# Attention in written order beside the product pairs: shared inner keys, narrower scores, raw zs

## The chip, the cores and the metric

The kernel runs on one core of one Trainium2 chip. What counts is the device time of one execution in microseconds (us), the median of the runs. TensorE is called PE (its weight loads PEld), VectorE DVE, ScalarE ACT, GpSimd POOL and SyncE SP, as the profile does. SBUF is the memory on the chip that all engines use; PSUM is the small memory of 8 banks into which PE writes; DRAM is outside.

## The reference, cut to what matters

One layer on 1024 tokens of width 1024, in float32. `h` is the normalised input; one projection gives queries `q` (16 heads of 64), keys `k` and values `v` (2 groups), and the gate inputs `za`, `u`, `vs`, `zs`, `gm`.

```python
a = window_sink_attention(q, k, v, att_sinks[l])
a = (a * jax.nn.silu(za)) @ w_att_out[l]
sgo = chunked_spatial_gating(gelu(u), gelu(vs), ...)
sgo = (sgo * jax.nn.silu(zs)) @ w_sg_out[l]
ga, gs = jnp.split(jax.nn.sigmoid(gm + b_merge[l]), N_BRANCHES, axis=-1)
x = x + (ga * a + gs * sgo) @ w_o[l]
```

In the attention each chunk of 64 queries sees its own 64 keys and the 128 before them, 192 in all; a learned sink per head joins the maximum and the denominator. A tile of 128 tokens holds two chunks: keys 0 to 191 of its window of 256 belong to the first, 64 to 255 to the second. So the 128 keys in the middle are seen by both, and the outer 64 on each side by one. In the first tile (t = 0) there is nothing before, and the chunks see 64 and 128 keys.

## The kernel before, in words

Everything is held transposed, features by tokens. Each product in float32 is made of three fp32r matmuls: an operand is split into a rounded part `hi` (a cast on ACT, L153) and a rest `lo` (a subtraction on DVE, L154), and `product` (L331) adds hi x hi, hi x lo and lo x hi over four blocks of 128: 12 matmuls of 512 columns.

Two blocks of 128 output features make a *pair* (`gemm_pair`, L348). A pair is a 2 x 2 block product with seven products instead of eight, named after their right-hand forms: `b11`, `t1`, `t2`, `b21`, `t3`, `b22`, `t4`. It needs seven left-hand blocks: the weights themselves (0, 1, 6) and four sums of them (2 to 5). Those sums are made on DVE (`sums`, L233) or, for some pairs, in DRAM by POOL's adding DMAs (`early_job`, L288). `split_next` (L206) splits the next unit of two blocks while the pair runs, four times a pair; a job's loads are issued by `begin_job` (L200). Results leave as four quarters, each through `finish`.

There are 33 pairs in this order: u (4), k and v (1), q (4), zs (4), the gates gs (4) and ga (4), za (4), the two output projections (8); then four pairs by tokens. The attention lies beside eleven of them: the last three of zs, and gs and ga. It has 32 steps, `steps` (L984): 2 key groups, 8 tiles, 2 parities of the heads, four heads each.

A step has three parts.

- `softmax_stage` (L1083): per chunk four score matmuls (two heads pairs, two parts of the split keys) over all 256 keys of the window into a bank `sc`; the minimum of the negated scores on DVE (L1106, L1107); four exponentials on ACT with their sums (L1109); the sink's; the reciprocal; and the scaling of the weights, half on DVE (L1128), half on ACT (L1130).
- `weight_stage` (L1133): per chunk and head pair one transpose of the first 128 keys (L1150) and one of the last 64 (L1161): 8 a step, 4 at t = 0; then splits of both banks `tp`.
- `value_stage` (L1166): per chunk two matmuls of 256 columns for the first 128 keys (hi and lo) and one for the last 64 (hi and lo stacked), L1183; the bank `o` is then put into `aT` by a copy on ACT (L1189) and an addition on DVE (L1190).

The order: `attention` (L1196) is a generator that yields after each part, and the pairs' hooks, seven a pair, call it by a credit (L1236). This only sets the order in which the program is traced; the framework's scheduler then orders the instructions of every engine itself, by that order as priority and by its own estimate of when each is ready, and gives out the buffers. Loads are issued on SP's queue, and stores too; POOL's queue carries `at_dr`, the adding DMAs (paced by L281 to follow an eviction) and some stores.

PSUM has two banks each of `mm`, `o`, `tp` and `sc`. In a pair `mm` holds the accumulator, `o` holds `t5` and `t2`, and the attention's values need `o` too.

zs: `zs_pair` (L1037) runs a pair, then applies Silu to its four quarters after the last exponentials traced so far (L1055 to L1060), loads the mixed rows `s1_dr`, multiplies on DVE (L1065) and stores `s_dr`, the input of the first output projection. Its forms are made on DVE and ACT (`forms_of`, L1306) at the end of za, whose pairs (L1336) apply Silu to their quarters, multiply by the attention `at_dr` and store `a_dr`.

## Time and profile before

| what | us |
|---|---|
| median of three runs (all: 937.09, 937.17, 937.66) | 937.17 |
| profiled execution, first to last instruction (span) | 935.4 |
| what a run has beside the span (937.17 - 935.4) | 1.8 |
| PE busy in it | 913.1 |
| DVE busy | 685.7 |
| ACT busy | 529.0 |
| first product of the eleven interleaved pairs to first of za | 320.4 to 618.7 |

The profile gives the span of the one execution that it took, not that execution's time as a run; the 1.8 us beside it are what the median has more. In a row of the timeline stand the start, the length, engine, line, operation, what is written and read, and how many were merged; in a row of a group the count, then busy us and the mean ns of one, then the engine's idle time before it and what ended it. A matmul's length contains its way through the array, so neighbours overlap, and the pace is read from starts.

### The profile page before, as it was taken

How to read it: one execution, taken by the hardware profiler on the slowest of the kernel's cores; microseconds unless marked ns; L12 is line 12 of the kernel's file. 1: busy time of each engine (PE TensorE's matmuls, PEld its weight loads, DVE VectorE, ACT ScalarE, POOL GpSimd, SP SyncE). 2: the span in 40 equal slices, each digit the busy share in tenths (PEclk: the TensorE clock that was granted, in tenths of full speed). 3: DMA queues.
4: the chain of work that ended last, by engine and by line, in shares of the span. 5: the costliest groups of instructions: out<-in, count | busy, mean ns of one | idle time of the engine just before them, and what ended most of it. 6: DMA issues, size and time to landing. Idle time of an engine off the chain costs nothing.

```text
span 935.4 us, 13276 instructions
## 1 busy us (share of the span) xinstructions
PE 913.1 (98%) x4393; PEld 758.6 (81%) x4393; DVE 685.7 (73%) x1214; ACT 529.0 (57%) x1031; POOL 128.2 (14%) x189
## 2 busy tenths in 40 slices
PE   7999999999999989999999999999999999999996
PEld 5788888888888778888888888888887887888885
DVE  5784776646678688787877877756598589679996
ACT  6873433334445468777757667744475475468443
POOL 1002222213011001111111111001110110210012
PEclk9999999999999999999999999999999999999998
DMA  6237679887788778897777778849668754998623
GB/s 251 99 113 212 215 183 190 163 156 220 240 282 265 222 231 220 186 229 195 207 217 240 242 176 231 235 162 371 234 207 313 268 202 155 293 307 289 204 101 124
DMA packets 129196, 202.24 MB, mean 216 GB/s; under 512 B 12680, under 2 KB 61064, under 8 KB 129128
## 3 DMA queue, kind: packets, MB, share of 16 engines
q1 hardware_dynamic: 109976, 148.69, 48.2%
q0 software_dynamic: 19008, 52.44, 23.7%
q8 instruction: 35, 0.57, 0.2%
q14 instruction: 33, 0.27, 0.1%
q10 hardware_dynamic: 144, 0.26, 0.1%
HBM read 144.59 MB, written 86.11 MB: 247 GB/s over the span
## 4 chain that ended last, share of the span: by engine, by line
PE 69%; DVE 15%; DMA 7%; issue 4%; ACT 3%; SPq 1%; POOL 0%; DVEq 0%; ACTq 0%
PE ps_mm L339 29%; PE ps_o L339 20%; PE ps_mm L564 5%; DVE wl L154 3%; PE ps_tp L339 2%; PE ps_sc L1098 2%; PE ps_o L1183 2%; DMA wr<-in_w_dram 2%; PE ps_tp L564 1%; PE ps_sc L564 1%; PE ps_o L564 1%; PE ps_tp L757 1%; DVE bq L183 1%; PE ps_tp L1150 1%; PE ps_tp L1161 1%
## 5 line engine op out<-in xcount | busy, mean ns | idle before, releaser
L153 ACT CAST wh<-s 128x1024 fp32r<-128x1024 f32 (+1 forms) x78 | 78.1, 1004 | 89.0 <-PE ps_mm L339 39.5
L153 ACT CAST wh<-wr 128x1024 fp32r<-128x1024 f32 (+1 forms) x80 | 66.3, 830 | 86.7 <-PE ps_mm L339 35.1
L154 DVE TENSOR_TENSOR wl<-wr,wh 128x1024 fp32r<-128x1024 f32 (+1 forms) x80 | 75.6, 947 | 51.4 <-ACT wh L153 51.0
L154 DVE TENSOR_TENSOR wl<-s,wh 128x1024 fp32r<-128x1024 f32 (+1 forms) x78 | 91.0, 1166 | 15.5 <-ACT wh L153 14.3
L1109 ACT ACTIVATE pr<-ps_sc,sm 128x192 f32<-128x192 f32 (+2 forms) x128 | 51.1, 411 | 33.8 <-DVE sm L1107 29.9
L339 PE MATMUL ps_o<-T_b22h,wh 128*128 128x512 f32 x148 | 59.0, 399 | 1.6 <-ACT x L361 1.6
L339 PE MATMUL ps_o<-T_t1h,wh 128*128 128x512 f32 x148 | 58.7, 396 | 0.3 <-ACT wh L153 0.2
L339 PE MATMUL ps_o<-T_b22l,wh 128*128 128x512 f32 x148 | 57.9, 391 | 0.0
L339 PE MATMUL ps_o<-T_b22h,wl 128*128 128x512 f32 x148 | 57.8, 390 | 0.0
L339 PE MATMUL ps_o<-T_t1h,wl 128*128 128x512 f32 x148 | 57.7, 390 | 0.0
L339 PE MATMUL ps_o<-T_t1l,wh 128*128 128x512 f32 x148 | 57.6, 390 | 0.0
L339 PE MATMUL ps_mm<-T_b11h,wl 128*128 128x512 f32 x140 | 54.8, 392 | 2.0 <-DVE wl L154 2.0
L339 PE MATMUL ps_mm<-T_t4h,wh 128*128 128x512 f32 x140 | 55.5, 397 | 0.7 <-DVE x L374 0.7
L339 PE MATMUL ps_mm<-T_t3h,wh 128*128 128x512 f32 x140 | 55.3, 395 | 0.0
L339 PE MATMUL ps_mm<-T_b11h,wh 128*128 128x512 f32 x140 | 55.1, 394 | 0.0
L339 PE MATMUL ps_mm<-T_t2h,wh 128*128 128x512 f32 x140 | 54.8, 392 | 0.0
L339 PE MATMUL ps_mm<-T_t4h,wl 128*128 128x512 f32 x140 | 54.7, 391 | 0.0
L339 PE MATMUL ps_mm<-T_t3h,wl 128*128 128x512 f32 x140 | 54.6, 390 | 0.0
L339 PE MATMUL ps_mm<-T_b11l,wh 128*128 128x512 f32 x140 | 54.6, 390 | 0.0
L339 PE MATMUL ps_mm<-T_t4l,wh 128*128 128x512 f32 x140 | 54.6, 390 | 0.0
L339 PE MATMUL ps_mm<-T_t2h,wl 128*128 128x512 f32 x140 | 54.6, 390 | 0.0
L339 PE MATMUL ps_mm<-T_t3l,wh 128*128 128x512 f32 x140 | 54.6, 390 | 0.0
(353 smaller groups left out, 2436.0 us busy)
## 6 DMA issues: line engine op xcount, KB each, us to landing
wr<-in_w_dram SPq DMA_DIRECT2D x86, 256.0 KB
sums<-in_w_dram POOLq DMA_DIRECT2D x20, 512.0 KB, 5.4
s<-sums SPq DMA_DIRECT2D x20, 512.0 KB
s_dr<-x SPq DMA_DIRECT2D x32, 256.0 KB
q_hl<-qhl SPq DMA_DIRECT2D x16, 512.0 KB
q<-q_hl SPq DMA_DIRECT2D x64, 128.0 KB
wr<-in_w_dram SPq DMA_DIRECT2D x14, 512.0 KB
y_dr<-x POOLq DMA_DIRECT2D x28, 256.0 KB, 6.3
```

Source lines behind the costliest of these rows:

```text
L153: nc.scalar.copy(hi, src)
L154: return nc.vector.tensor_sub(lo, src, hi.bitcast(F32))
L183: op(dst[:, i : i + 2, :], a[:, i : i + 2, :], c[:, i : i + 2, :])
L339: nc.tensor.matmul(acc, lt, rt, start=fresh and k == 0 and n == 0, stop=k == 3 and n == 2, skip_group_check=True,)
L564: mm = nc.tensor.matmul(acc, lt, rt, start=k == 0 and n == 0, stop=k == KC - 1 and n == 2)
L757: nc.tensor.matmul(pm[:, t * P : (t + 1) * P], xh[:, half * 4 + t, g * P : (g + 1) * P], bias[-1][1][:, g % 4, :], start=True, stop=True,)
L1098: nc.tensor.matmul(sc[:, i, k0:], q_of[:, c, i * P : (i + 1) * P], kt[:, f, k0:], start=f == 0, stop=f == 1,)
L1109: nc.scalar.activation(pr[:, c, i, 0 : hi - lo], sc[:, i, lo:hi], AF.Exp, bias=nmax[:, c, i : i + 1], scale=-1.0, accum_out=sums[:, c, i : ...
L1150: nc.tensor.transpose(pt[:, at : at + P], pr[:, c, i, 0:P], ident[:])
L1161: nc.tensor.transpose(pt[0:64, at : at + P], pr[:, c, i, first : first + 64], ident[:])
L1183: nc.tensor.matmul(po[:, cs], lt, rt, start=n == 0, stop=n == len(terms) - 1)
```

## The change

1. **Written order.** In the eleven pairs `locked_pair` replaces `gemm_pair` and the generator. Inside `tc.manual_schedule` PE, ACT and DVE run their instructions as written; SP and POOL are still scheduled. With a, b, c, d for four steps in a row (d is the next pair's a), PE's order in a pair is: values of the step before a, `b11`, transposes of a, scores of b, `t1`, values of a, `t2`, transposes of b, `b21`, scores of c, `t3`, values of b, `b22`, transposes of c, scores of d, `t4`.
2. **Shared inner keys.** The weights of both chunks lie in one tile of 384 columns per head pair. The 128 inner keys are transposed four times (two chunks, two head pairs) into one bank, and the outer keys of both chunks, side by side, twice into another. The values are two matmuls of 512 columns for the inner keys and one of 256 per chunk for the outer.
3. **192 keys of scores.** A score matmul covers only its chunk's 192 keys (64 and 128 at t = 0, as columns of the window).
4. **zs raw.** The three zs pairs store their quarters unchanged in `zr_dr`. In the first two za pairs `gate_raw` loads six rows of it with `s1_dr`, applies Silu on ACT, multiplies on POOL and stores `s_dr`; the s quarters are loaded from za's third pair on instead of the second, one each hook instead of every second. The first zs pair still multiplies on DVE, but applies Silu at once, quarter by quarter.
5. **Weight sums.** gs and ga (8 jobs) and the first two of each output projection get their sums from DRAM; za's and the third and fourth of the first projection's are now made on DVE. DVE's sums are made in two halves, at places of their own. Locked pairs split a pair's third unit inside that pair rather than ahead of it.
6. **Queues.** The `a_dr` stores of za's first two pairs go on SP's queue, not POOL's.

```diff
+        ends = mtile([P, 2, 3 * HD], F32R, "v", 2, aheads)
+        k = max(t - 1, 0) * P
+        both = rows[k : (t + 1) * P].rearrange("(c p) d -> p c d", p=64)
         for e in range(2):
-            nc.sync.dma_start(vb[e * 64 : (e + 1) * 64].bitcast(F32), own)
+            nc.sync.dma_start(ends[e * 64 : (e + 1) * 64].bitcast(F32), both[:, :: both.shape[1] - 1, :])
...
                     nc.tensor.matmul(
-                        sc[:, i, k0:],
+                        sc[:, i, lo:hi],
                         q_of[:, c, i * P : (i + 1) * P],
-                        kt[:, f, k0:],
+                        kt[:, f, lo:hi],
...
+    def turn(n):
+        st = held[n]
+        st.wide = wide = P if st.t else 64
+        st.inner = bank("tp")
         for c in range(2):
+            for i in range(2):
+                at = (2 * c + i) * P
+                nc.tensor.transpose(
+                    st.inner[0:wide, at : at + P], st.pr[:, i, place_of(c, 64 if st.t else P, 192)], ident[:]
+                )
+        st.ends = bank("tp")
+        for i in range(2):
+            nc.tensor.transpose(st.ends[0:wide, i * P : (i + 1) * P], st.pr[:, i, P : P + wide], ident[:])
...
+        if st.t:
+            terms = [(inner[:, vs], st.a[:, i, :], slice(0, HALF)) for i in range(2)]
+        else:
+            terms = [(ends[:, 0, vs], st.a[:], slice(0, HALF))]
+        for c in range(0 if st.t else 1, 2):
+            terms.append((ends[:, c, vs], st.b[:, cols(c)], cols(c)))
...
+        of(values, a - 1)
+        acc = bank("mm")[:]
+        mm(acc, 0, "b11", True)
+        of(weigh, a)
+        for tail in tails:
+            tail()
+        tails.clear()
+        of(outputs, a - 1)
+        if p:
+            make_sums(None, 1)
+        if by_dve and p:
+            begin_job()
+
+        of(turn, a)
+        of(scores, b)
+        t5 = bank("o")[:]
+        mm(t5, 2, "t1", True)
+        x11 = xtile()
+        pace[0] = nc.scalar.copy(x11[:], acc)
+        of(casts, a)
+        of(inner_rest, a)
+        of(maxima, b, 0)
+        of(ends_rest, a)
+        of(maxima, b, 1)
+        of(exponentials, b)
+
+        of(values, a)
+        mm(acc, 3, "t2", False)
+        of(weigh, b)
+        of(outputs, a)
+        x22 = xtile()
+        pace[0] = nc.scalar.mul(x22[:], t5, -1.0)
+        if p:
+            split_next()
+            if not by_dve:
+                begin_job()
+
+        of(turn, b)
+        t2 = bank("o")[:]
+        mm(t2, 1, "b21", True)
+        x12 = xtile()
+        pace[0] = nc.scalar.copy(x12[:], acc)
+        of(casts, b)
+        of(inner_rest, b)
+        of(ends_rest, b)
+        split_next()
+        make_sums(None, 1 if p else 2)
+
+        of(scores, c)
+        mm(acc, 4, "t3", False)
+        nc.vector.tensor_add(x11[:], x11[:], t2)
+        finish(0, 0, x11, x11[:], 1.0)
+        of(maxima, c, 0)
+        of(maxima, c, 1)
+        split_next()
+        of(exponentials, c)
+
+        of(values, b)
+        mm(t5, 5, "b22", False)
+        of(weigh, c)
+        nc.vector.tensor_sub(x22[:], x22[:], acc)
+        finish(1, 1, x22, x22[:], 1.0)
+        of(outputs, b)
+
+        of(turn, c)
+        of(scores, d)
+        mm(acc, 6, "t4", False)
+        nc.vector.tensor_add(x12[:], x12[:], t5)
+        finish(0, 1, x12, x12[:], 1.0)
+        hold = split_next(True)
+        of(casts, c)
+        of(inner_rest, c)
+        of(maxima, d, 0)
+        of(ends_rest, c)
+        of(maxima, d, 1)
+        hold()
+        of(exponentials, d)
+        tails.append(lambda: finish(1, 0, xtile(), acc, -1.0))
...
+    with tc.manual_schedule(engines={mybir.EngineType.PE, mybir.EngineType.Activation, mybir.EngineType.DVE}):
+        p = 0
+        for dst in (zr_dr, gs_dr, ga_dr):
+            for m in range(2 if dst is zr_dr else 0, KC, 2):
+                locked_pair(p, rest(dst, m))
+                p += 1
...
+        for j in range(2, KC):
+            yield
+            z = raws.pop(j)
+            nc.scalar.activation(z[:, 0:2, :], z[:, 0:2, :], AF.Silu)
+            if j + 3 < KC:
+                load_raw(j + 3)
+            yield
+            nc.gpsimd.tensor_tensor(z[:, 0:2, :], z[:, 0:2, :], z[:, 2:4, :], op=ALU.mult)
+            copy_to(s_dr[j * P : (j + 1) * P, :], z[:, 0:2, :].rearrange("p h n -> p (h n)"))
```

`weigh` is the scaling of the weights with what leads to it, `maxima` the minima on DVE, `exponentials` ACT's part; `casts` makes the hi parts of both transposed banks (one cast for the inner keys, one of 64 partitions for each chunk's outer ones), `inner_rest` and `ends_rest` the lo parts; `outputs` puts the values' bank into `aT`. `split_next(True)` makes only the cast and hands back the subtraction, to be placed later (`hold()`).

More of the change, by code (lines that the diff above doesn't have):

```diff
@@ L1166, in value_stage @@
[L1166 to L1188 removed]
+                    nc.scalar.mul(v, v, st.inv[:, c, i : i + 1])
@@ new lines, in ends_of, with casts @@
+    def ends_of(st):
+        return ((1, slice(0, 64), slice(64, P)), (0, slice(64, P), slice(0, 64)))[: 2 if st.t else 1]
+    def casts(n):
+        st = held[n]
+        if st.t:
+            st.a = atile([P, 2, HALF], F32R, "pT", 2)
+            nc.scalar.copy(st.a[:, 0, :], st.inner[:])
+        else:
+            st.a = atile([P, HALF], F32R, "pT", 2)
+            nc.scalar.copy(st.a[0:64, :], st.inner[0:64, :])
+        st.b = atile([P, HALF], F32R, "pTb", 2)
+        for c, hi, lo in ends_of(st):
+            nc.scalar.copy(st.b[hi, cols(c)], st.ends[hi, 0:256])
@@ new lines, in outputs, with locked_pair, of, mm @@
+                st.at[:],
+            )
+            if n + 3 < len(steps):
+                value_loads(*steps[n + 3][:2])
+        del held[n]
+    held = {}
+    tails = []
+    def locked_pair(p, finish):
+        a, b, c, d = range(3 * p - 1, 3 * p + 3)
+        def of(make, n, *rest):
+            if 0 <= n < len(steps):
+                make(n, *rest)
+        def mm(acc, at, form, fresh):
+            product(acc, ready[n, at], hb[form], fresh)
+            part_of_early(1 if p < 3 else 2)
+        n = done[0]
+        done[0] += 1
+        by_dve = n + 1 not in ahead_of
+        of(values, a - 1)
[70 more added lines that the diff above has]
+        tails.append(lambda: finish(1, 0, xtile(), acc, -1.0))
@@ L1251, in hybrid_tile @@
+    begin_job()
     assert not early
@@ L1338, in hybrid_tile @@
             want_gates(at_dr, m)
-        if m == 2:
+            next(gating)
+        if m == 4:
+            for _ in gating:
+                pass
             s_q = {}
```

357 lines of the change are left out of this document (168 added, 189 removed).

## The prediction

> **What bounds the kernel now.** The page first: which engine has no room, and at what clock.
>
> ```profile
> span 935.4 us, 13276 instructions
> ...
> PE 913.1 (98%) x4393; PEld 758.6 (81%) x4393; DVE 685.7 (73%) x1214; ACT 529.0 (57%) x1031; POOL 128.2 (14%) x189
> ...
> PEclk9999999999999999999999999999999999999998
> ```
>
> PE is busy 98% of the span at the full clock in every slice; DVE and ACT have about a quarter and two fifths to spare. A busy share may hide waiting, so next the busy time by stretch. The first row is the eleven interleaved pairs (the first `T_b11h` of the second zs pair to the first one of za), the next two are za's four pairs; the columns are length, busy us (and instructions) of PE, PEld, DVE, ACT and POOL, clock, DMA share, GB/s. The last row is the fullest DMA stretch I found.
>
> ```profile
> 320.40:618.70 298.30, 293.78 (x1599) 249.66 (x1598) 231.18 (x519) 209.67 (x557) 36.61 (x47) 1.00 0.77 214
> 618.70:656.80 38.10, 38.10 (x170) 31.55 (x169) 20.23 (x25) 16.39 (x24) 4.03 (x7) 1.00 0.86 310
> 656.80:694.90 38.10, 38.10 (x170) 31.53 (x169) 25.17 (x30) 23.45 (x31) 4.30 (x8) 1.00 0.60 205
> 640.00:645.00 5.00, 5.00 (x23) 4.13 (x23) 3.89 (x4) 1.19 (x2) 0.07 (x1) 1.00 1.04 407
> ```
>
> DVE works 231 and ACT 210 of 298.3 us in the eleven pairs, so there PE is the limit as long as the order of the work lets it run. What PE's time consists of is read from the chain of work that ended last and from PE's timeline, by distances between starts (a matmul's own duration overlaps the next one's).
>
> ```profile
> 112.22 2.72 PE ps_o L339 x12
> ```
>
> Twelve 512-wide matmuls, one product, take 2.72 us. Eleven pairs of seven products: 77 x 2.72 = 209.4 us. The attention's instructions, in the timeline of the step near 504 us:
>
> ```profile
> 504.40 0.60 PE L1150 MATMUL ps_tp<-ident,pr 128*128 128x128 f32 x4
> 504.84 0.60 PE L1161 MATMUL ps_tp<-ident,pr 128*64 128x128 f32 x4
> 505.19 1.21 PE L1098 MATMUL ps_sc<-k,q 128*128 128x256 f32 x8
> 506.24 0.40 PE L339 MATMUL ps_mm<-T_t4h,wh 128*128 128x512 f32 x1
> ```
>
> Four transposes take 504.84 - 504.40 = 0.44, so 0.109 each. From 504.40 to the next product's start at 506.24 is 1.84; without eight transposes (0.87) it leaves 0.97 for eight 256-wide score matmuls, 0.121 each. Value matmuls (256 wide), and score matmuls of a first tile (128 wide):
>
> ```profile
> 347.64 0.28 PE L1183 MATMUL ps_o<-pTb,v 128*128 128x256 f32 x1
> 347.76 0.40 PE L1183 MATMUL ps_o<-pT,v 128*128 128x256 f32 x2
> 348.00 0.39 PE L339 MATMUL ps_mm<-T_b11h,wh 128*128 128x512 f32 x1
> ```
>
> ```profile
> 322.66 1.05 PE L1098 MATMUL ps_sc<-k,q 128*128 128x128 f32 x8
> 323.55 0.45 PE L339 MATMUL ps_o<-T_t1h,wh 128*128 128x512 f32 x1
> ```
>
> The values: 0.36 for three, 0.120 each. The narrow scores: 0.89 for eight, 0.111 each: half the columns, almost the same time.
>
> There are 32 steps (2 key groups x 8 tiles x 2), 4 of them with t = 0. Now: scores 28 x 8 x 0.121 + 4 x 8 x 0.111 = 30.7; values (28 x 6 + 4 x 3) x 0.120 = 21.6; transposes (28 x 8 + 4 x 4) x 0.109 = 26.2; together 78.5. So 298.3 - 209.4 - 78.5 = **10.4 us are neither**: waiting and the change from one kind of matmul to another. The waits of PE's weight loads name most of it (us, times, longest):
>
> ```profile
> PEld ps_o L339 <- DVE aT L1190: 3.7, 6, 1.3
> PEld ps_o L339 <- ACT x L361: 2.0, 1, 2.0
> PEld ps_o L1183 <- DVE x L369: 1.9, 6, 0.5
> PEld ps_sc L1098 <- ACT pr L1109: 1.5, 4, 1.0
> ```
>
> These are banks held by `aT` and `x` evictions, and exponentials that come late.
>
> **The change, part by part.** *Less PE work.* The 128 keys that both chunks see are turned once for two 256-column blocks that lie side by side, and the two outer 64-key blocks share one transpose per head pair: 6 transposes a step instead of 8 (6 instead of 4 at t = 0), so 32 x 6 x 0.109 = 20.9, a gain of 5.3. The values become two 512-wide and two 256-wide matmuls a step (one and one at t = 0): a 512-wide one is 2.72 / 12 = 0.227, so 60 x 0.227 + 60 x 0.120 = 20.8, a gain of 0.8. The scores go from 256 to 192 columns. The trace has no 192; its bounds are the 256-wide row (0.121, no gain) and the 128-wide one (0.111, a gain of 224 x 0.010 = 2.2). I take 0.118, a gain of 0.7, since halving the columns gave so little. Sum: 78.5 - 6.8 = 71.7.
>
> The Trainium skill bears on this ("TensorE: Matmul & The Clock Gate", section "Back-to-back issue gap"): an isolated warm matmul needs N / 2.4 + 2.5 ns, thus 82.5 for 192 columns and 109 for 256, which would make the scores' gain 6.0 us by an estimate from that page. This case's trace disagrees, 111 ns where the formula gives 56 for 128 columns; the same page's section "LDWEIGHTS" (128 columns at 1.2 GHz, 107 ns) agrees with it.
>
> *The written order.* PE, ACT and DVE now run the eleven pairs in a fixed order, three steps a pair: a pair's PE work is 7 x 2.72 + 3 x 2.29 = 25.9. The question is what PE waits for. Between a step's scores S and its transposes T the order puts two products and one step's values (2 x 0.227 + 2 x 0.120 = 0.69): 6.13 us, for each of the three steps. In that time its softmax must pass DVE and ACT. One softmax now, DVE then ACT:
>
> ```profile
> 462.64 1.03 DVE L1106 TENSOR_REDUCE sm<-ps_sc 128x2 f32<-128x384 f32 x2 [0.18 <-PE ps_sc L1098]
> 465.69 0.16 DVE L1120 TENSOR_TENSOR sm<-sm,sm 128x4 f32<-128x4 f32 x1 [1.62 <-ACT sm L1119]
> 466.10 0.55 DVE L1128 TENSOR_SCALAR pr<-pr,sm 128x192 f32<-128x192 f32 x2
> ```
>
> ```profile
> 463.84 0.42 ACT L1109 ACTIVATE pr<-ps_sc,sm 128x192 f32<-128x192 f32 x1 [1.07 <-DVE sm L1107]
> ...
> 465.44 0.22 ACT L1119 ACTIVATE sm<-sm 128x4 f32<-128x4 f32 x1
> ...
> 466.16 0.80 ACT L1130 ACTIVATE pr<-pr,sm 128x192 f32<-128x192 f32 x2
> ```
>
> From 462.64 to 466.16 + 0.80 it takes 4.3. What else stands on these queues in the gap, with its price:
>
> ```profile
> L154 DVE TENSOR_TENSOR wl<-s,wh 128x1024 fp32r<-128x1024 f32 x24 | 29.3, 1222 | 7.1 <-ACT wh L153 5.9 <-PE ps_sc L1098 1.1
> L154 DVE TENSOR_TENSOR pT<-ps_tp,pT 128x512 fp32r<-128x512 f32 x28 | 19.2, 685 | 1.9 <-ACT pT L153 1.6
> L369 DVE TENSOR_TENSOR x<-x,ps_o 128x512 f32<-128x512 f32 x11 | 7.5, 685 | 1.6 <-PE ps_o L339 1.2
> L240 DVE TENSOR_TENSOR s<-wr 128x512 f32<-128x512 f32 x10 | 6.8, 682 | 0.0
> L154 DVE TENSOR_TENSOR pTb<-ps_tp,pTb 64x256 fp32r<-64x256 f32 x4 | 1.7, 418 | 0.1
> ```
>
> ```profile
> L153 ACT CAST wh<-s 128x1024 fp32r<-128x1024 f32 x24 | 25.1, 1045 | 15.2 <-PE ps_mm L339 8.2 <-PE ps_o L339 6.3 <-DVE s L241 0.6
> L153 ACT CAST pT<-ps_tp 128x512 fp32r<-128x512 f32 x28 | 16.4, 586 | 1.7 <-PE ps_tp L1150 1.4
> L1055 ACT ACT_TABLE_LOAD x4 | 5.1, 1283 | 0.1
> L1109 ACT ACT_TABLE_LOAD x4 | 5.1, 1283 | 0.9 <-DMA s_dr<-x 0.4 <-DVE sm L1107 0.4
> ```
>
> Step b: the previous step's inner rest (0.69) ahead and its two outer rests (2 x 0.42) between the two minima: 4.3 + 1.5 = 5.8 of 6.13. Step c: the term into `x11` (0.69) ahead: 5.0; ACT's split of 1.05 falls beside the minima. Step d: inner rest, outer rests, and on ACT the held split (1.05) and three casts (0.59 + 2 x 0.38), of which some precede S: 5.8 to 6.5. So the waits lie between 0 and 0.4 us a step. Whole queues fit: DVE about 20 of 25.9 a pair, ACT about 19.6. In the first two pairs and the last, DVE also makes weight sums (0.68 each, two to four a pair); in the other eight they now come from DRAM, made by POOL's adding DMAs, which takes 8 x 2.7 us off DVE and adds about 0.75 MB of loads a pair at a DMA share of 0.77. Eight ACT table loads (10.2 us of ACT, the two last rows) shrink to the one from Silu to Exp, since no Silu is left among the exponentials; the zs results go straight out and hold no `x` tile for a gate. PE did not wait for ACT's throughput, so I count this only as part of the waits. I take 0.2 us a step, 6.4 in all, between 0 and 0.8 (a step's chain that overruns its gap by 0.4 twice). **Stage: 209.4 + 71.7 + 6.4 = 287.5, a gain of 10.8.**
>
> *What is moved to za.* Six raw rows are loaded (1 MB each with `s1`), passed through Silu on ACT (1.05 each, ACT has 16.4 of 38.1 in use), multiplied on POOL and stored. POOL's price of such a multiply is not in the trace; the nearest row is a subtract of the same size:
>
> ```profile
> 8.98 2.37 POOL L580 TENSOR_TENSOR T_t1l<-T_t3h,T_t1h 128x1024 fp32r<-128x1024 f32 x1 [7.53 <-ACT T_t1h L579]
> ```
>
> 6 x 2.4 = 14.2 of 38.1 us: POOL has the room, and nobody waits for it but the s quarters, which load a pair later than now, all four in the first four hooks of za's third pair. DVE also makes za's sums, 2.7 a pair, beside 20.2 of 38.1. The stores of `a_dr` move from POOL's queue to SP's, where the raw loads, the gates and the next weights stand behind a store that waits for DVE; a late weight has a whole pair of cover (its split is needed 11 us into the pair, its product at 19). DMA in the first two za pairs: 6 MB raw, 3 stored, 2 gates, 2 of `a_dr`, 2 weights = 15 MB in 38.1 us = 394 GB/s, against 310 now and 407 in the fullest stretch. It just fits, so the price lies between 0 and, if the quarters come 5 us late and the s forms with them, 5. I take 1.0.
>
> Before the eleven pairs the sums are only split in two and the order of POOL's early DMAs changes; PE has no wait there to lose, and I count nothing (cover: the DVE's idle quarter; without it 0.7 a product).
>
> *Sum.* The profiled execution has a span of 935.4, and the median of the three runs, 937.17, lies 1.8 above it. -10.8 + 1.0 = -9.8: span 925.6, **927.4 us**.
>
> **The rivals.**
>
> *Clean order*: the gaps hold and PE changes over for nothing: remainder 0 to 2, stage about 282.5, gain 15.8: 922.4 with the 1.0 of za. For it: no chain above is longer than its gap by more than 0.4. Against it: S, T and V are many small groups, and today a remainder stays too where nothing is named.
>
> *Scores by their columns*: if only columns counted, 192 of them would take 192 / 512 x 0.227 = 0.085, a gain of 224 x 0.036 = 8.1 instead of 0.7: 920.0. Against it is the 128-wide row, 0.111 where columns alone would make it 0.057; nothing in the trace is for it. (This is what the issue-gap rule of the Trainium skill's page, named above, would do here.)
>
> *Late s forms*: za at its DMA limit costs the 5, so 931.4. For it: 394 of 407 GB/s. Against it: the quarters are first cast when za's last pair has freed its forms, a pair after their issue. The Trainium skill has a rule against POOL's multiply ("SBUF — State Buffer", section "Who interferes with whom"): a DVE instruction with two SBUF inputs and a GpSimd one that reads SBUF shut each other out for their whole length. No run here shows the pair. As a mechanism of this kernel it takes up to 14.2 us from DVE in those two pairs, 20.2 + 5.5 + 14.2 = 39.9 of 38.1: DVE becomes their limit by about 2 us, and the result is 929 to 930, within this rival.
>
> *The order is too tight* (slower): the chain S to T runs through some six hand-overs between DVE and ACT in fixed queues, and an instruction that comes late (a weight that has not landed ahead of the exponentials, a bank not free) delays every one behind it; the scheduled order of before could put other work there. Place: the gap from the fourth scores (before `t4`) to their transposes in the next pair. It decides where a step waits more than (298.3 - 1.0 - 281.1) / 32 = 0.51 us; at 0.7 the stage takes 303.5: 943.4.
>
> *Narrow scores are slow*: two passes per column below 256, so 192 columns at 2 x 192 / 512 x 0.227 = 0.170 instead of 0.121: +11.0 against no gain, +11.7 against my sum: 939.1. Against it the first narrow score of a tile, whose weights were already in:
>
> ```profile
> 322.66 0.22 PE L1098 MATMUL ps_sc<-k,q 128*128 128x128 f32 x1
> ```
>
> 0.22 against 0.28 for 256 and 0.39 for 512 columns: one rate for all widths, so the floor is the weight load, not the column.
>
> **Chances.** Forecast (924.5 to 930): 0.48. Late forms (930 to 935.3): 0.14. Clean order (below 924.5): 0.14. Scores by columns: 0.02. Too tight an order: 0.15, narrow scores: 0.03. Gains and losses that cancel: 0.04. A measurement of this kernel can tell 0.2% (1.9 us) from no change, so faster 0.78, same 0.04, slower 0.18. The range takes in the clean order down to 921 and reaches up to 940, past the break-even and the cheaper of the two slow cases, with about 0.09 left above and 0.09 below.
>
> **What would show it.** Right: transposes 192 at 0.109; 192-wide scores eight in 0.94; from the first product of the eleven pairs to the first of za 284 to 291 us; at most two or three table loads there. The order fails if PE's waits name `pr` (the scaled weights) or `aT` dozens of times, or a split ahead of the exponentials waits for a `wr` or `s` DMA. Za fails if PE's wait at the first sg pair (now 1.7 us at 712 to 715) grows, with the first cast of a form ended by a DMA. I am wrong altogether if the pair's length, 25.9 and some tenths, is not what the middle pairs show.

## The result: slower by 0.6%, and the profile after

| | before | after |
|---|---|---|
| median of four runs, us | 937.41 (937.09 to 938.25) | 942.44 (940.39 to 946.31) |
| span of the profiled execution, us | 935.4 | 938.4 |

The ratio is 1.0057, 95% interval 1.0034 to 1.0080: slower, outside the forecast's 924.5 to 930 and outside its range. A profile shows one execution, for the changed kernel the shortest of its four (940.39 us) and, among the experiments below, for the multiply on DVE, no late gating and no gating at all the longest, so a span or a wait of one trace need not be the median's: 3.0 us between the spans stand here for 5.0 between the medians. The page of the profile after, the rows that answer to those of before:

```profile
span 938.4 us, 13120 instructions
...
PE 909.4 (97%) x4285; PEld 751.4 (80%) x4285; DVE 691.8 (74%) x1222; ACT 529.7 (56%) x1050; POOL 150.3 (16%) x199
...
PEclk9999999999999999999999999999999999999998
```

PE is less busy by 3.7 us and the span is longer by 3.0: PE waits more, and part of the busy time is spent at a lower clock. Where, is seen in busy time by stretch. The eleven pairs begin in both traces with the first `b11` product at 316.1; the first row is theirs before, the second after (to za's first product), the next two are za's four pairs, the last two stretches of 5 us with a lowered clock.

```profile
316.10:618.70 302.60, 297.34 (x1613) 252.22 (x1613) 235.48 (x528) 211.40 (x559) 36.61 (x47) 1.00 0.76 213
```

```profile
316.10:612.60 296.50, 290.21 (x1505) 244.89 (x1504) 223.41 (x515) 204.91 (x570) 43.20 (x57) 0.99 0.87 236
612.60:657.60 45.00, 40.41 (x170) 32.04 (x168) 26.57 (x28) 21.51 (x29) 16.66 (x7) 0.96 0.92 340
657.60:697.70 40.10, 39.10 (x169) 31.42 (x170) 33.21 (x39) 23.46 (x31) 3.33 (x6) 1.00 0.84 300
320.00:325.00 5.00, 2.99 (x8) 2.30 (x9) 5.00 (x11) 2.04 (x4) 0.00 (x0) 0.75 0.57 182
635.00:640.00 5.00, 4.68 (x13) 3.28 (x14) 5.00 (x5) 1.43 (x2) 2.39 (x1) 0.66 0.99 342
```

The eleven pairs: 302.6 to 296.5, a gain of 6.1 where 10.8 was forecast (302.6 is more than the prediction's 298.3 because the stretch begins 4.3 us earlier: the last product of the first zs pair, `t4`, lies inside it in both traces). Za's four pairs: 76.2 (two rows of 38.1 before) to 85.1, a loss of 8.9 where 1.0 was forecast. -6.1 + 8.9 is +2.8, nearly the 3.0 of the spans.

*Inside the eleven pairs* the forecast pace is there. A step in PE's timeline, its six transposes, eight scores and the next product:

```profile
503.37 0.60 PE L1180 MATMUL ps_tp<-ident,pr 128*128 128x128 f32 x4
503.80 0.38 PE L1185 MATMUL ps_tp<-ident,pr 128*128 128x128 f32 x2
503.94 1.17 PE L1109 MATMUL ps_sc<-k,q 128*128 128x192 f32 x8
504.95 0.42 PE L351 MATMUL ps_mm<-T_t4h,wh 128*128 128x512 f32 x1
```

From 503.37 to 504.95 is 1.58 us, against 1.84 for the same stretch before. From the fourth pair to the tenth a pair takes 25.8 to 26.2 us by its starts; 25.9 was forecast without waits. What is missing stands at the beginning, again in PE's timeline:

```profile
318.60 0.39 PE L351 MATMUL ps_mm<-T_b11h,wl 128*128 128x512 f32 x1
321.75 0.31 PE L1109 MATMUL ps_sc<-k,q 128*128 128x64 f32 x1 [2.76 <-DMA q<-q_hl]
322.31 0.66 PE L351 MATMUL ps_mm<-T_t4h,wh 128*128 128x512 f32 x1 [0.26 <-DVE x L386]
322.77 0.63 PE L351 MATMUL ps_mm<-T_t4l,wh 128*128 128x512 f32 x1
323.19 0.63 PE L351 MATMUL ps_mm<-T_t4h,wl 128*128 128x512 f32 x1
```

The first score waits 2.8 us for the first query tile, and then product matmuls start 0.43 us apart instead of 0.23, at a granted clock of 0.75 over that stretch. Before, the first scores came at 322.66, after the last product of the first zs pair; now one of them stands ahead of it. By the distances of starts the wait is 2.9 us, and with some 2.1 us in the slow matmuls behind it the loss is 5.0.

*In za*, DVE's and POOL's timelines and PE's waits (us, times, longest):

```profile
629.37 2.48 DVE L1491 TENSOR_TENSOR x<-x,g 128x512 f32<-128x512 f32 x1 [2.24 <-ACT x L1490]
631.78 3.38 DVE L156 TENSOR_TENSOR wl<-wr,wh 128x1024 fp32r<-128x1024 f32 x1
635.08 2.85 DVE L1491 TENSOR_TENSOR x<-x,g 128x512 f32<-128x512 f32 x1
637.86 0.67 DVE L390 TENSOR_TENSOR x<-x,ps_o 128x512 f32<-128x512 f32 x1
638.46 1.21 DVE L156 TENSOR_TENSOR wl<-s,wh 128x1024 fp32r<-128x1024 f32 x1
```

```profile
628.90 8.49 POOL L1472 TENSOR_TENSOR bq<-bq 128x1024 f32<-128x1024 f32 x3 [13.73 <-DMA bq<-s_dr]
```

```profile
PE ps_mm L351 <- DVE wl L156: 3.4, 2, 2.9
PE ps_mm L351 <- ACT wh L155: 1.6, 1, 1.6
```

While POOL multiplies (628.9 to 637.4), a DVE operation of 0.7 us takes 2.5 and 2.9, and one of 1.2 takes 3.4; after it they have their old lengths. The next weights' `lo` is late, PE waits 2.9 us and loses clock: about 5 us by the distances of starts. The Trainium skill's rule ("SBUF — State Buffer", "Who interferes with whom": DVE with two SBUF inputs and a GpSimd instruction that reads SBUF exclude each other) agrees with these rows. At 657.6 to 662 PE waits again, 1.6, 0.5 and 0.4 us of idle time (3.3 us by the distances of starts to 663); with the place above that makes about 8 of the 8.9 us. SP had issued the weights for these products behind other things:

```profile
631.33 0.32 SPq L201 DMA_DIRECT2D s_dr<-bq  x1
...
641.21 0.48 SPq L201 DMA_DIRECT2D s_dr<-bq  x1
642.04 0.38 SPq L478 DMA_DIRECT2D a_dr<-x  x1
642.62 0.32 SPq L201 DMA_DIRECT2D g<-at_dr  x1
643.30 4.26 SPq L201 DMA_DIRECT2D wr<-in_w_dram  x4
```

### The profile page after: what moved, and what is told of

It reads as the page before. It is cut to its first block, busy times and chain, and to the rows that moved or that the text cites. A ratio compares the mean times of both kernels' runs of the same rounds, so it can differ in the third digit from the quotient of the medians.

```text
span 938.4 us, 13120 instructions
## 1 busy us (share of the span) xinstructions
PE 909.4 (97%) x4285; PEld 751.4 (80%) x4285; DVE 691.8 (74%) x1222; ACT 529.7 (56%) x1050; POOL 150.3 (16%) x199
## 4 chain that ended last, share of the span: by engine, by line
PE 46%; DMA 8%; DVE 6%; issue 3%; ACT 2%; SPq 0%; POOL 0%; ACTq 0%; DVEq 0%; POOLq 0%
PE ps_mm L351 20%; PE ps_o L351 15%; PE ps_sc L1109 3%; PE ps_sc L351 2%; PE ps_o L1233 2%; PE ps_tp L351 2%; DMA q<-q_hl 2%; DMA g<-at_dr 1%; PE ps_tp L1180 1%; DVE wl L156 1%; DMA wr<-in_w_dram 1%; DMA s_dr<-bq 1%; DMA bq<-zr_dr 1%; DVE bq L185 1%; DMA v<-v_dr 1%
## 5 line engine op out<-in xcount | busy, mean ns | idle before, releaser
L156 DVE TENSOR_TENSOR wl<-wr,wh 128x1024 fp32r<-128x1024 f32 (+1 forms) x80 | 77.9, 975 | 50.6 <-ACT wh L155 49.8
L155 ACT CAST wh<-s 128x1024 fp32r<-128x1024 f32 (+1 forms) x67 | 66.4, 996 | 83.5 <-PE ps_mm L351 32.4
L156 DVE TENSOR_TENSOR wl<-s,wh 128x1024 fp32r<-128x1024 f32 (+1 forms) x67 | 77.9, 1164 | 19.2 <-ACT wh L155 19.1
L306 POOL DMA_DIRECT2D sums<-in_w_dram x48 | 36.3, 957 | 148.4 <-PE ps_mm L587 64.0
L351 PE MATMUL ps_mm<-T_t2l,wh 128*128 128x512 f32 x140 | 54.6, 390 | 0.0
```

Source lines behind the costliest of these rows:

```text
L155: nc.scalar.copy(hi, src)
L156: return nc.vector.tensor_sub(lo, src, hi.bitcast(F32))
L306: return lambda: paced(nc.gpsimd.dma_start(dst, src, accum_op=op))
L351: nc.tensor.matmul(acc, lt, rt, start=fresh and k == 0 and n == 0, stop=k == 3 and n == 2, skip_group_check=True,)
```

## The experiments

All are edits of the changed kernel unless said otherwise; a ratio is against the kernel before on the same chip, with its 95% interval. A step (hook) is one of the seven calls between a pair's products. My theory: order and PE savings do what was forecast, and the gating of zs in its new place (8.9 us) and the first queries (5.0 us, where the queries wait for their transfer) take it back. Rivals: the written order is too tight; the narrow scores cost; the DMA engines alone are the price in za.

### What the late gating costs

**No late gating.** The locked zs pairs store straight into `s_dr`, and `gate_raw` goes.

```diff
-                locked_pair(p, rest(dst, m))
+                locked_pair(p, rest(s_dr if dst is zr_dr else dst, m))
```

> The changed kernel without the late gating: the locked zs pairs store zs raw into the rows that the sg and za stages read, and the za pairs load, apply and multiply nothing of it (this leaves Silu(zs) * s1 out for the rows 256 to 1023). Theory: all of what the za stage lost, 85.1 against 76.2 us for its four pairs, comes from this work, through the port, the transfers and ScalarE together: 942.4 - 8.9 = 933.5 us, with the za pairs at 76-77 us. Against the run with the multiply on VectorE it prices loads and Silu (3-4 us). Rival: the za stage is slow for a reason that the late gating has no part in (weights that are no longer made ahead of time): 940-943 us, za pairs above 83 us.

Measured: 933.60, ratio 0.9945 (0.9928 to 0.9962). Za's stretches:

```profile
617.10:655.30 38.20, 38.20 (x171) 31.60 (x171) 26.53 (x35) 16.76 (x23) 0.75 (x1) 1.00 0.86 291
655.30:693.40 38.10, 38.10 (x170) 31.55 (x169) 27.34 (x34) 23.60 (x31) 3.27 (x6) 1.00 0.54 178
```

76.3 us, PE without a wait. The whole loss in za is the late gating's (this kernel leaves it out, loads, Silu, multiplies and stores together), and the sums that DVE now makes there cost nothing.

**The multiply on DVE.**

```diff
-            nc.gpsimd.tensor_tensor(z[:, 0:2, :], z[:, 0:2, :], z[:, 2:4, :], op=ALU.mult)
+            nc.vector.tensor_mul(z[:, 0:2, :], z[:, 0:2, :], z[:, 2:4, :])
```

> The changed kernel with one edit: the six late multiplies of Silu(zs) by s1 in the za pairs run on VectorE instead of GpSimd. Theory (port): while GpSimd multiplies, VectorE's own operations stretch from 0.7 to 2.5-2.9 us and from 1.2 to 3.4 us, the next weights are late and TensorE waits 3.2 us at 635 us and then runs at a lower clock. On VectorE a multiply costs about 1.2 us, so the 3.2 us wait and the clock loss behind it go: 942.4 - 5.0 = 937.4 us, and no VectorE subtraction in the za pairs above 1.5 us. Rival (transfers): the late weights come from the DMA engines, which are full there; then the wait at 635 stays and the time stays within 1 us of 942.4. Rival (VectorE has no room): the multiplies queue ahead of the splits on VectorE, new waits of about 1 us each take the place, 940-943 us.

Measured: 941.34, ratio 1.0030 (1.0013 to 1.0046); za 82.6 us. DVE's rows there:

```profile
635.34 1.23 DVE L1472 TENSOR_TENSOR bq<-bq 128x1024 f32<-128x1024 f32 x1 [3.21 <-ACT bq L1468]
636.48 0.69 DVE L1491 TENSOR_TENSOR x<-x,g 128x512 f32<-128x512 f32 x1
637.08 1.22 DVE L156 TENSOR_TENSOR wl<-wr,wh 128x1024 fp32r<-128x1024 f32 x1
```

No operation is stretched, so the stretching was POOL's; but of 5.0 us only 2.5 come back, from 85.1 to 82.6 in za; the ratio falls by as much, 0.0027, which alone is no more than its uncertainty. Waits of 0.9 and 0.8 us (idle time) take part of the place, and those at 662 stay.

**Loads and stores of the gating on POOL's queue**, with the multiply on DVE; then **two steps later** as well.

```diff
-            copy_to(z[:, at : at + 2, :]..., src[j * P : (j + 1) * P, :])
+            nc.gpsimd.dma_start(z[:, at : at + 2, :]..., src[j * P : (j + 1) * P, :])
```

> The changed kernel with the six late multiplies on VectorE, and the loads of zs raw and s1 for them and the stores of their products issued by GpSimd's queue and not SyncE's. Theory (queue order): in the run with the multiply on VectorE alone, SyncE stood for the first product's store from 631 to 636.6 us and the next pair's weights, behind it, were issued at 649.5-654.6 us; in the run without gating they went out by 646 us, and the waits of 1.89, 0.80, 0.65 and 0.34 us (3.7 us) at 662-667 us were absent. Off SyncE's queue the 3.7 us go: 941.3 - 3.7 = 937.6 us, the four za pairs at about 79 us against 82.6. Rival (bytes): the weights are late because the DMA engines are full with the extra 6 MB, whoever issues; the 3.7 us stay and the time is 940-942 us.

> The run above, and the late gating starts two steps later in the first za pair (step three in place of one; its last multiply then falls at the last step of the second pair). Theory: with the multiply on VectorE, ScalarE's first late Silu stood 4.2 us for its load at 630-634 us with the casts of the next weights behind it, and TensorE waited 1.14, 1.08 and 0.35 us at 637-640 us; started later, the load has landed and these 2.6 us go too: 935 us with both, the za pairs at 76.5-77.5 us, as in the run without gating. Rival (VectorE and ScalarE have no room for six more operations each): the waits move to the second pair, 937-938 us.

Measured: 944.89, 1.0073 (1.0055 to 1.0091), and 944.50, 1.0067 (1.0043 to 1.0091). Za takes 86.9 and 90.0 us, and both theories fell in this form. In the first run the waits at 662 went, but one of 2.8 us came at 653, and at 629 ACT stood for the first raw row with a copy and a cast for PE behind it (waits of ACT and PE):

```profile
ACT L1468 <- DMA bq<-zr_dr: 6.0, 1, 6.0
...
PE ps_mm L351 <- ACT x L376: 6.8, 2, 4.1
```

**Gating in place**: three of the four quarters are gated in the tiles from which the forms are made, spread over three za pairs, all on DVE and POOL's queue (a rewritten `gate_raw`).

> The changed kernel; the late gating of three of the four quarters is done in place, in the tiles from which the next stage's forms are made, so that only one quarter is stored and loaded again: 9 MB of transfers for it in the za stage in place of 13 (the kernel without late gating has 4). The multiplies are on VectorE, the transfers on GpSimd's queue, and the steps are spread over three za pairs in place of two. Theory (transfers and the queueing behind them are the price): the za pairs fall from 85.1 us to 78-80 us, 935-938 us in all. Rival (the price is the six Silu and six multiplies in the engines' own order, which are all still there): 82 us for the za pairs as in the run with the multiply on VectorE, 941 us.

Measured: 950.95, ratio 1.0118 (1.0103 to 1.0133); za 94.7 us. Fewer bytes and more waiting: ACT stood for loads again, and PE's waits there are 5.9, 4.4 and 2.5 us.

```profile
ACT bq L1465 <- DMA bq<-zr_dr: 13.7, 3, 7.0
...
ACT L1465 <- DMA bq<-zr_dr: 7.9, 1, 7.9
```

So bytes alone are not the price, though this edit also moves the loads to POOL's queue and the steps over three pairs.

**Gating in the attention pairs**: `finish` collects a zs pair's four quarters; Silu for all four behind the next pair's first product, the multiplies in two batches.

> The changed order, but the three locked zs pairs are gated in the attention stage: the four quarters of a pair get their Silu on ScalarE behind the next pair's first product, in one batch, and their multiply by s1 on VectorE in two batches later in that pair; nothing of zs is stored raw, loaded or multiplied in the za pairs. The arithmetic is whole. Theory: the za stage is then as without late gating, 76 us for its four pairs, and the order of the attention pairs is not what costs. In the pairs the batch takes two table loads of 1.28 us and four Silu of 0.6 us on ScalarE (18.9 of 26.2 us busy) and 2.7 us on VectorE (19.7 of 26.2): 1 to 2 us of waits for each of three pairs on top of the 933.6 us without late gating, 936-939 us. Rival (the written order has no room for a batch of 5 us on ScalarE): the exponentials behind it come 4-5 us late each time, TensorE waits and loses clock, 945-950 us.

Measured: 947.70, ratio 1.0102 (1.0073 to 1.0130). Za is whole again, but the three pairs behind a gated one take 32 + 32 + 30 us in place of 27 + 27 + 26. The rival's time came true: at this place the written order has no room for 5 us on ACT.

### What the first queries wait for

**Queries ahead of the rotation**, taking steps of their own; then **in one step**; then also the **first zs pair's stores on POOL's queue**.

```diff
-    steps_of_q += [rotate(1, 1), first_loads()]
+    steps_of_q += [first_loads(), rotate(1, 1)]
```

> The changed kernel with one edit: in the first zs pair the steps that load the first two query tiles go ahead of the step that rotates the last queries. Theory: the first scores stand 2.95 us for the query transfer at 318.8-321.7 us and the next nine matmuls of 512 columns then take 0.2 us more each at a lower granted clock; with the queries fetched earlier both go: 942.4 - 5.0 = 937.4 us, eleven pairs starting like the later ones. Rival (the tile waits for a free place or for the rotated queries, not for its place in the queue): no change, 942 us. Rival (the clock drop in the first pairs belongs to something else than the wait): only the wait goes, 939.5 us.

> The changed kernel; in the first zs pair the first two query tiles are loaded ahead of the rotation, but in the same step, so that the rotation runs at the step where the changed kernel has it. In the earlier run that took two steps more for this, the first scores did not wait, but the transposes behind them waited 10.75 us: the first maxima on VectorE and the first exponentials on ScalarE stood until stores of the stage before had landed, which SyncE issued behind the rotation's eight stores. Theory: without the two steps, those stores go out about as early as in the changed kernel, the wait for the queries (2.9 us and 2.1 us of clock) goes and the wait of the transposes grows to at most 3 us: 942.4 - 5 + 1.9 = 939 us, between 937.4 and 941. Rival: the first exponentials are bound to the end of the first zs pair, so that the 5 us come back whole in front of the transposes: 942 us or more.

> The run above, and the four stores of the gated first zs pair are issued by GpSimd's queue, so that they do not stand behind the rotation's stores on SyncE's. Theory: what the first maxima and exponentials wait for is the landing of these stores; issued at once they land some 3 us earlier and the transposes wait 1 us or less: 1 to 3 us less than the run above, 937-938 us. Rival: they wait for the rotation's stores themselves (the tiles of the attention take the place of the tiles that these read): no difference from the run above.

Measured: 947.57, 1.0095 (1.0074 to 1.0116); 948.08, 1.0110 (1.0088 to 1.0131); 950.39, 1.0132 (1.0117 to 1.0148). The first scores no longer wait, but the transposes behind them do, 10.5, 5.5 and 7.7 us, and in the second and third run the `t1` product too, 4.0 and 5.2 us. My account of why fell with the third run. DVE's waits in the second and the third:

```profile
DVE x L1074 <- DMA rot<-s_dr: 5.3, 1, 5.3
```

```profile
DVE x L1074 <- DMA rot<-s_dr: 8.8, 1, 8.8
```

The last multiply of the first zs pair stands for its gate, which SP loads behind the rotation's eight stores (327.99 us in the second run); the first minima stand behind it on DVE. What went ahead on SP here pushed this gate back.

**No gating at all** (also none in the first zs pair):

```diff
-    gemm_pair(hb, gate_of_zs, part_of_zs)
+    gemm_pair(hb, rest(s_dr, 0), part_of_q)
```

> The changed kernel without any gating of zs: neither beside za nor in the first zs pair (this leaves Silu(zs) * s1 out for all rows; zs goes raw into the rows that the next stage reads). Theory: the order of the eleven pairs brings what was predicted for it, and what eats it is the gating in its two new places. In the first zs pair its gate loads (0.75 MB) are issued ahead of the queries' and its multiplies stand ahead of the first maxima on VectorE; without them the first scores wait 1 us or less: 933.6 - 5 + 1 = 929.6 us, near the 927.4 that was predicted for the whole change. Rival: the first scores wait for the queries because the order has them earlier than the kernel before (ahead of the last product of the first zs pair), with the gates or without: 933-934 us, first wait still 3 us.

Measured: 931.56, ratio 0.9921 (0.9891 to 0.9952). This lies between the two. A wait of 4.5 us at 323 is still there in the traced execution (this time in the product that ends the first zs pair, for an operand that stands on DVE behind the rotation's loads), so a wait at this place does not need the gate loads. Two adding transfers are issued ahead of it here as well, at 310.95.

**Adding transfers one pair later.** These weight sums are not due in the first pair.

```diff
-            part_of_early(1 if p < 3 else 2)
+            if p:
+                part_of_early(1 if p < 4 else 2)
```

> The changed kernel; GpSimd's accumulating transfers that make sums of later weights begin one pair later (none in the first of the eleven pairs, one at each product in the second to fourth). In the changed kernel the first two of them are issued at 309-311 us, in the kernel before none between 286 and 335 us; behind them the DMA engines are 0.90 busy at 221 GB/s in 315-320 us against 0.60 at 150, and the queries and the rows of the rotation take 7 to 8 us to land. Theory: these two take the DMA engines; without them the first scores wait 1 us or less and the clock stays: 942.4 - 4 = 938.4 us. Rival (the scores simply stand earlier than the queries can be there: loads issued at 311-314 us land at 321-322 whatever else runs): the wait stays at 3 to 4 us, 942 us.

Measured: 940.11, ratio 1.0013 (0.9997 to 1.0030). DMA share and GB/s are the last columns; the changed kernel first, then its POOL, then this run:

```profile
315.00:320.00 5.00, 3.99 (x18) 2.98 (x16) 2.80 (x5) 1.33 (x2) 0.00 (x0) 1.00 0.90 221
```

```profile
309.33 1.80 POOL L306 DMA_DIRECT2D sums<-sums  x2 [23.41 <-ACT x L376]
```

```profile
315.00:320.00 5.00, 4.13 (x20) 3.19 (x19) 5.00 (x11) 3.22 (x5) 0.00 (x0) 1.00 0.68 169
```

The first score comes at 317.81 without a wait. The other traces agree: in the eight that load the queries as the changed kernel does and have the early adding transfers and the gating of the first zs pair, the first score waits 2.8 to 4.6 us; in the six with the transfers later, 0 to 1.2. So the cause of this wait is the two adding transfers beside the first queries. But part of it moves: in those six the transposes behind wait 1.4 to 2.4 us at 330 to 332 (1.1 at most in the eight), and here a wait of 1.9 us for later queries appears at 379, where the transfers now are. From the first pair's start to the fifth's the changed kernel's trace takes 114.4 us, and this one takes 114.4 as well; the 4 us by which the ratio is lower are not seen in this pair of traces.

### The narrow scores, and the parts together

> The changed kernel with the scores' matmuls at their old width: 256 columns of keys (128 in the first block) in place of 192. Theory, from the two traces: a matmul of 192 columns follows the one before after 118 to 120 ns and one of 256 after 119, so the narrowing brings nothing: 942.4 us within 1 us. Rival (time by columns): 25 per cent of about 105 ns for 256 matmuls come back, 6.7 us: 949 us. The prediction's own term for it, 0.7 us, lies within the first.

Edit: `sc[:, i, 0 if t else P :]` and `kt[:, f, 0 if t else P :]` for `lo:hi`. Measured: 942.68, ratio 1.0049 (1.0031 to 1.0068), the same as with 192. Narrowing neither helps nor hurts.

**Multiply on DVE and queries ahead of the rotation**, together.

> Both edits: late multiplies on VectorE, and the first queries loaded ahead of the rotation. Theory: the two costs lie in different stages and add up, 942.4 - 5.0 - 5.0 = 932.4 us, faster than the kernel before (937.4). Rival (transfers): only the part of the queries goes, 937.4. Rival (written order too tight): neither helps, 940-943.

Measured: 944.29, 1.0062 (1.0045 to 1.0078); better than the queries ahead alone (1.0095), and still slower than the kernel before.

**Adding transfers one pair later and gating in place**, together.

> The two runs above together. If both theories hold, 942.4 - 4 - 6 = 932 us, faster than the kernel before (938); if only the second, 936-938; if neither, 941 or more.

Measured: 948.08, 1.0086 (1.0071 to 1.0101): 3 us better than the gating in place alone; the later adds by themselves brought 4.

**The two edits that had helped**, multiply on DVE and later adds, with the adds spread; to it the stores on POOL's queue; to that the start two steps later.

```diff
+            if p:
+                part_of_early(2 if p < 7 else 1)
```

> The changed kernel with two edits: no accumulating transfers in the first of the eleven pairs, then one at every second product up to the seventh and one at every product in the last four (in the run before, one pair later at every product, the wait of the first scores was gone and one of 2.1 us had come at 379 us, where these transfers then were); and the late multiplies on VectorE. Measured alone against the kernel before, the changed kernel had 1.0057, the adds one pair later 1.0013 and the multiply on VectorE 1.0030. Theory: the gains add, and the 2.1 us at 379 us go as well: 1.0057 - 0.0044 - 0.0027 - 0.002 = 0.997, 935.5 us. Rival (waits only move): 1.000, 938.5 us.

> The run above, and the stores of the late products are issued by GpSimd's queue, so that SyncE does not stand for a product with the next weights behind it (the loads stay on SyncE's). Theory (SyncE's order makes the weights at 656-663 us late): the waits of 1.9, 0.8, 0.65 and 0.34 us go: 3.7 us less than the run above, 932 us. Rival (the weights are late for the transfers' sake): the same time as the run above.

> The run above, and the late gating starts two steps later. Theory (ScalarE's first Silu stands for its load with casts behind it, 4.2 us at 630-634 us with the multiply on VectorE): the waits of 1.1 and 1.1 us of the first za pair go as well, 2 us less than the run above. Rival: the waits move to the second pair, within 1 us of the run above.

Measured: 937.99, 0.9996 (0.9977 to 1.0015); 937.76, 1.0000 (0.9982 to 1.0017); 937.91, 0.9996 (0.9976 to 1.0016). The first gains add, within the intervals. From the first pair's start to the fifth's these three and the next run take 110.1 to 112.3 us, against 114.4 to 120.4 in the eight traces above with the early adds (the one that gates in these pairs left aside) and 114.4 and 115.8 in the two with the adds one pair later: spreading the adds is what shortens this stretch. The other two edits change nothing: za takes 82.4, 82.4 and 83.1 us, with the waits elsewhere each time. The place of the stores in SP's order alone is not the price, and neither is the first step's place in ACT's.

```diff
+            if p and (7 * p + at) % 3:
+                part_of_early(1)
```

> The run with the multiply on VectorE and the stores of the late products on GpSimd's queue, but with the accumulating transfers spread evenly: none in the first of the eleven pairs, then at two of every three products in the other ten (in that run one at every second product up to the seventh pair and one at every product in the last four, where waits of 0.3, 1.5 and 1.8 us of the scores for their queries had come at 534, 562 and 590 us). Theory (these transfers push the queries late where they are dense): the waits in the last three pairs go and none of over 1 us comes in the others: 937.8 - 3 = 935 us, 0.997 of the kernel before. Rival: a wait for the queries comes wherever a transfer falls beside their load; the same time as that run, 1.000.

Measured, on the run with stores on POOL's queue: 936.66, ratio 0.9986 (0.9972 to 1.0000), the fastest of the kernels that compute the whole layer, and at most just faster than before. PE's waits from the first pair to za's end:

```profile
PE ps_sc L1109 <- DMA q<-q_hl: 3.6, 3, 1.3
PE ps_mm L351 <- DVE x L386: 2.0, 1, 2.0
PE ps_tp L1180 <- DMA wr<-in_w_dram: 1.4, 1, 1.4
PE ps_mm L351 <- DVE wl L156: 1.3, 2, 0.8
```

The longest wait for queries is 1.3 us. Za still takes 83.2.

## Why the prediction was wrong, point by point

- **Less PE work**: right. By an estimate from the counts of each shape in the two traces, each at its usual distance of starts, the whole execution has about 6 us less of it (forecast 6.8). Transposes run at 0.108 to 0.109. The scores' 0.7 is not there: 192 columns take as long as 256, shown by the run with the old width. So the rival by columns and the rival of slow narrow scores both fell.
- **The written order**: right in the middle, and the slower rival, an order too tight, is not what happened: 25.8 to 26.2 us a pair against 25.9, while that rival needed 0.5 us of wait a step. What PE loses against its undisturbed pace in the stage is about 12 us by the same estimate, 5.0 of them at the first score; the other 7 were forecast as 6.4.
- **The first scores** were the first step that failed: nothing was counted, and the loss is 5.0 us. "Before the eleven pairs ... the order of POOL's early DMAs changes; PE has no wait there to lose, and I count nothing." The order of those DMAs did cost: they share the DMA engines with the first queries, and the order has the first score stand ahead of a product that used to cover the queries' landing. Shown by the run with the adds one pair later (no wait of the first score, ratio lower by 0.0044, 4 us) and by the two groups of traces; that the missing cover of a product has a part in it is argued from the order alone.
- **Za** was the second: "It just fits, so the price lies between 0 and ... 5. I take 1.0." It is 8.9, and with all late gating gone the whole kernel is 0.0112 of the time before, 10.5 us, better than the changed one (each ratio with about 0.2% of its own). I summed bytes and busy time and looked for who waits for the result; what costs is who stands behind the work. One way is shown by an edit: DVE stretched under POOL's multiply (the stretched rows go, and 2.5 us come back with the multiply on DVE). Two more are seen in the traces, ACT standing for a raw row and SP standing for a product, but taking one of them away brought nothing. I had priced the port rule of the Trainium skill as 2 us of DVE's throughput; here its price is latency, a weight that PE waits 2.9 us for. The sign that the prediction named for za, PE's wait at the first sg pair, hardly moved (1.0 and 0.6 us after, 0.9 and 0.2 before): the loss came in za's own products.
- These two steps are the miss: za lost 7.9 us more than forecast, and the eleven pairs gained 4.7 less, about the 5.0 at the first score. Together that is 12.6 of the 12.8 us between the forecast span of 925.6 and 938.4.
- **The clock** was missing from the forecast altogether: both waits of some 3 us are followed by slow matmuls, so that each costs about 5.
- Open: why za takes 82 us or more wherever the gating was put beside it (82 to 95 in the traces). Single orders and bytes are ruled out one by one; that in-order waits on ACT, DVE and SP trade places under busy DMA engines is what the waits show in each run, but no placement was found that proves it by making za short with the gating in. No run loads the raw rows beside za without using them, so the transfers by themselves have no price yet.

Nor does the order alone reach its forecast: without any gating, which the kernel before does and this one leaves out, the time is 0.9921 of the time before, 7.4 us less, where -10.8 was forecast.

## What to carry to other kernels

Moved work that "has room" by busy time and bytes still stands in some engine's order: list for each moved instruction what it waits for and which casts, copies or loads for the bottleneck stand behind it, and price that wait, not its length. When an order puts the bottleneck's instruction earlier, ask whether its transfer was covered by what it now overtakes, and what other transfers begin beside it. In this kernel a wait of PE of about 3 us has to be priced with the slow matmuls after it.

## What the runs showed of the hardware that I had not expected

Over all twenty traces, from 100 us on and counted as idle time of PE: each of the 31 waits longer than 2.3 us had 4 to 12 matmuls at 0.43 us instead of 0.23 behind it, 0.8 to 2.4 us more; between 1.7 and 2.2 us some had and some had not (1.86 at 663 us in the run with the gating's loads and stores on POOL's queue two steps later had not, 1.92 at 357 us in the run without late gating had); of lone waits of 1.2 to 1.65 us none. The traces' granted clock is 0.50 in these places, for 3.41 us at a time (322.50 to 325.91 and 636.52 to 639.93 in the changed kernel's) or two to four times as long. The Trainium skill ("TensorE: Matmul & The Clock Gate", "Part 1: The HAM clock gate (the "warmup" mystery)") puts the limit at an idle window of about 3.4 us; here waits of 2.3 are enough.

The changed kernel's four runs spread over 6 us and the first four of the kernel before over 1.2. But 29 runs of the kernel before, beside the run with the adds spread, spread over 5.2 (936.71 to 941.95), so the spread is not the change's alone. The mean granted clock in the three shortest of these 29 is 0.998 and in the three longest 0.992; that the clock makes the spread is argued from this, not tried.
